# Token-major branches and gates, and state-space tables stored without a mask, in a two-block decoder kernel

## The chip, the cores and the metric

The kernel runs on one core of a Trainium2 chip. It is one program with one launch. The metric is the device time of one execution in microseconds; a profiled execution gives a trace of each engine's instructions beside it. The engines are TensorE (PE, with its weight loads PEld), the vector engine (DVE), ScalarE (ACT), GpSimd (POOL) and the queue of SyncE (SP), which issues most DMAs.

## The reference

256 tokens of width 2048 go through two blocks, in fp32. Cut to what the change touches:

```python
# block 1: three mixers, each with a gate of full width
gates = sigmoid(gate_logits).reshape(B, S, 3, D)           # from h @ w_in
mixed = (gates[:, :, 0] * (o_a @ w_branch_a) + gates[:, :, 1] * (o_b @ w_branch_b)
         + gates[:, :, 2] * (o_c @ w_branch_c))
x = x + rms_norm(mixed @ w_out, g_post_mix)
...                                                         # then a gated feed-forward layer
# block 2, first layer: a state-space mixer, 128 groups of 16 channels with 64 states
x_t = a * x_{t-1} + bb @ u_t;  y_t = Re(c @ x_t) + d * u_t  # an associative scan over 256 tokens
# block 2, second layer: attention with 16 heads in 4 groups, three branches each
o = sum over 3 branches of (sigmoid gate) * silu(z) * o_branch      # z from h @ w_qg
y = o.reshape(B, L, 2048) @ w_o
```

The three attention branches are attention over 15 compressed blocks, over selected blocks and over a window; with 256 tokens the last two are causal attention with keys and values of their own.

## The kernel before

Every large product takes its fp32 weights from HBM in units of two rows of 128 and 512 columns (512 KB, tile `raw`). `unit` (line 173 on) loads one on SP's queue; `split` turns it into a rounded high half `whi` (ScalarE, line 156) and a remainder `wlo` (vector engine, line 157), and three matmuls per product (high by high, high by low, low by high) are done at TensorE's fast fp32 rate. There are 4 buffers of `raw` and 3 of each half. Activations live as `Act`: feature-major, 128 features on the partitions and 256 tokens beside, as high and low halves.

Two functions multiply. `ws` is feature-major: the weights are stationary, 256 tokens move, and the result has features on the partitions. `as_` is token-major: 128 tokens of the activations are stationary, 512 weight columns move, and the result has tokens on the partitions. Both work on a unit at a time and call `pump` after it, which lets side work advance: generators for attention, retention, the state-space tables and the modulation vectors (in the background, `BACK`), each of which yields a cost that is charged against a rate per unit. `late` holds functions that `as_` calls before its second or third unit (`do_late`); the feed-forward layer uses it to transpose its token-major result (`transpose_act`, line 796) into an `Act`. A scheduler orders each engine's instructions by a simulated timeline, so program order and order in the trace differ in detail.

- `branch` (line 805 on) runs once for each of the three mixers. For four blocks of 512 columns it computes gates and the branch's product with `ws`, applies tanh on ScalarE, multiplies and adds into `mixed` (two tiles of 8 x 256), and for the last mixer splits the halved sum into the `Act` `mx`, which `post_norm` multiplies by `w_out`.
- `ssm_tables` (line 1124 on) builds the state-space tables beside the feed-forward layer. At its end eight steps multiply `bT` by the table `gm` (in DRAM, loaded 8 groups at a time by `group_tile`) into a PSUM tile whose four strips of 32 partitions are filled one after the other; ScalarE copies them, the vector engine adds the skip term, and GpSimd's queue writes `kern` (DRAM, 128 groups x (112 zeros + 16 x 128)), line 1297.
- `ssm` projects `u` (token-major) and then `z` (feature-major, 32 units). Beside the units of `z` run `ssm_states`, then `ssm_direct` and `ssm_scan` together, then `ssm_before` and `ssm_out`. `ssm_direct` (line 1577 on) loads each group's table from `kern` as overlapping windows, a Toeplitz matrix; in a row of 8 steps `s` the window runs into the channel before, so GpSimd multiplies the tile by the mask `past` (line 1588):

```python
nc.sync.dma_start(raw, bass.AP(tensor=self.kern.tensor, offset=self.kern.offset + g * 2160,
                               ap=[[16, 128], [2160, 8], [1, 128]]))
nc.gpsimd.tensor_mul(raw, raw, cols(past, 8))
```

- `ssm_scan` is a serial chain of 30 steps with four small vector instructions each (lines 1545 to 1548); `ssm_before` copies its result (line 1560), and `ssm_out` multiplies it by `gm`, loaded again.
- `nsa` multiplies, for each of four head groups, three blocks of gates `z` by the attention's outputs, feature-major; `nsa_attention` runs one group ahead as side work and leaves its outputs feature-major, with the values (`vc`, `vsw`) stationary and 4 x 128 columns of transposed probabilities moving.

GpSimd's instructions run in order, its DMA issues among them: after the last write of `kern` it multiplies `y` by the norm's gain (line 938) at the end of the feed-forward layer, and then makes the low halves of the first weights of `ssm` (`as_first`).

Of the kernel before, what the change touches and what calls it, by code (L numbers as in the profile page):

```python
# [17 lines left out]
OP = mybir.AluOpType  # L18
# [55 lines left out]
class Kernel:  # L74
# [115 lines left out]
    def ws(self, act, wv, c0, j=None, before=None, quiet=False, shared=False):  # L190
# [3 lines left out]

        nk = act.n
        ps = [self.mp.tile([128, 2, S], F32, name=f"mm{i}") for i in range(2)]
        for k0 in range(0, nk, 2):
# [8 lines left out]
            if before is None and not quiet:  # L206
                self.pump()
        return ps
# [596 lines left out]
    def branch(self, i, o, w, mixed, act=None, done=None):  # L805

        nc = self.nc
        win = self.a["w_in"].rearrange("o (k p) n -> p (o k) n", p=128)
        wv = w.rearrange("o (k p) n -> p (o k) n", p=128)
        for b in range(4):  # L810
            ps = self.ws(self.hT, win, GATE + i * D + b * 512)
            gs = []
            for q in range(2):
                g = self.work([128, 2, S], "big")
                nc.scalar.activation(g, ps[q], AF.Tanh, scale=0.5)
                gs.append(g)
            ps = self.ws(o, wv, b * 512)
            for q in range(2):
                k = b * 4 + q * 2
                m = mixed[k // 8].t[:, k % 8:k % 8 + 2]  # L820
                g = gs[q]
                if act is None:
                    nc.vector.scalar_tensor_tensor(m, g, 1.0, ps[q], op0=OP.add, op1=OP.mult)
                else:
                    nc.vector.scalar_tensor_tensor(g, g, 1.0, ps[q], op0=OP.add, op1=OP.mult)
# [169 lines left out]
    def first(self):  # L995
# [25 lines left out]
        mixed = [self.slot([128, 8, S], F32, "mixed") for _ in range(2)]  # L1021
# [29 lines left out]
        for m in mixed:  # L1051
            m.free()
        self.BACK = 0.2
        xs, h2, ready, ss = self.post_norm(mx, a["w_out"], a["g_post_mix"], a["x"][0])
# [70 lines left out]
    def ssm_tables(self):  # L1125
# [9 lines left out]
        self.kern = dp.tile([128, 112 + 16 * 128], F32, name="kern")  # L1135
# [109 lines left out]
        nc.gpsimd.dma_start(self.kern[:, :112], zero)  # L1245
# [37 lines left out]

        for t in range(8):
            p = self.ps([128, 4, 128], "sc", 1)
            for l in range(4):
                if l % 2 == 0:
                    raw = self.group_tile(self.gm.rearrange("g r n w -> g (r n) w"), t * 16 + l * 4)
                for q in range(4):
                    self.mm(p[l * 32:l * 32 + 16, q], bT.t[:, :, t * 16 + l * 4 + q], raw[:, l % 2 * 4 + q], True, True)  # L1290
            k = self.work([128, 4, 128], "side")
            for l in range(4):
# [3 lines left out]
                dst = self.kern[t * 16 + l * 4:t * 16 + l * 4 + 4, 112:]  # L1296
                nc.gpsimd.dma_start(dst.rearrange("q (c w) -> c q w", c=16), k[r])
# [687 lines left out]
```

## Time and profile before

| | |
|---|---|
| median of 3 runs (lowest, highest) | 3266.39 us (3265.74, 3269.41) |
| the profiled execution's own time | 3265.34 us |
| its span, first to last instruction | 3263.2 us |
| mean granted TensorE clock | 0.989 |
| HBM read, written | 716.80 MB, 24.24 MB |

A profile line gives a group of instructions by line, engine and operation, what it writes from what, and how often; then busy time, mean time of one, and the idle time of the engine before it with what ended it. In the timeline equal instructions in a row are merged (x4) under the start of the first and the time from there to the end of the last. Matmuls are pipelined: a record lasts longer than the distance to the next start. An fp32 product that is not in halves shows as two records.

### The profile page before, as it was taken

Reading aid. Unit: us, or ns where it says so; the run is one execution under the profiler, and the core shown is the slowest. Engines: PE = TensorE matmul, PEld = TensorE weight load, DVE = VectorE, ACT = ScalarE, POOL = GpSimd, SP = SyncE. Lnnn points to the kernel's source line nnn. Section 1 sums busy time; section 2 is a strip of 40 time slices with the busy share of each in tenths; the row PEclk is TensorE's granted clock in tenths of the full one; section 3 lists DMA queues with packets and bytes.
Section 4 is the critical chain, followed back from the end, with each engine's and each line's share of the span. In section 5 each row is a group of like instructions: output and inputs, shape, how many; then the busy total and the mean of one; then the engine's idle time right before and its main releaser. Section 6 shows DMA issues by size and latency. Waiting matters only on the chain. (4 is left out here: it accounts for less than half of the span.)

```text
span 3263.2 us, 52186 instructions
## 1 busy us (share of the span) xinstructions
PE 3166.2 (97%) x20582; PEld 2812.7 (86%) x20582; DVE 2375.1 (73%) x3580; ACT 1461.9 (45%) x2066; POOL 177.2 (5%) x184
## 2 busy tenths in 40 slices
PE   9999999999999998999999999898899899999998
PEld 8999899988999996887778778677798798899997
DVE  7777676777787766999989956757777865655666
ACT  5544434344344445444434444554444434544444
POOL 0000000000000002000000010303100200000000
PEclk9999999999999999999999999898999999999999
DMA  8868756888777785677777788486788585455574
GB/s 280 260 196 270 237 184 200 255 279 270 223 235 246 249 286 160 213 273 251 262 264 272 253 279 272 139 273 199 232 240 268 170 272 174 135 150 161 143 229 171
DMA packets 438246, 744.48 MB, mean 228 GB/s; under 512 B 29732, under 2 KB 105288, under 8 KB 437104
## 3 DMA queue, kind: packets, MB, share of 16 engines
q1 hardware_dynamic: 428000, 710.45, 68.4%
q0 software_dynamic: 9360, 29.62, 2.6%
q8 instruction: 161, 2.64, 0.3%
q10 hardware_dynamic: 640, 1.07, 0.1%
q14 instruction: 85, 0.70, 0.1%
HBM read 716.80 MB, written 24.24 MB: 227 GB/s over the span
## 5 line engine op out<-in xcount | busy, mean ns | idle before, releaser
L156 ACT CAST whi<-raw 128x1024 fp32r<-128x1024 f32 (+2 forms) x1059 | 1029.5, 981 | 1375.8 <-PE mm L150 1191.3
L157 DVE TENSOR_TENSOR wlo<-raw,whi 128x1024 fp32r<-128x1024 f32 (+2 forms) x1045 | 1181.6, 1139 | 611.3 <-ACT whi L156 600.0
L150 PE MATMUL mm<-act,whi 128*128 128x256 f32 (+1 forms) x8000 | 1485.0, 287 | 3.7 <-ACT whi L156 3.7
L150 PEld LDWEIGHTS mm<-act,whi 128*128 128x128 f32 (+1 forms) x8000 | 1255.5, 193 | 34.7 <-issue 24.3
L150 PE MATMUL mm<-whi,act 128*128 128x512 f32 x3792 | 1185.1, 391 | 5.4 <-ACT whi L156 4.5
L150 PE MATMUL mm<-act,wlo 128*128 128x256 f32 (+1 forms) x4000 | 1143.7, 288 | 7.0 <-DVE wlo L157 6.9
L150 PEld LDWEIGHTS mm<-whi,act 128*128 128x128 f32 x3792 | 711.4, 188 | 160.6 <-issue 7.0
L150 PEld LDWEIGHTS mm<-act,wlo 128*128 128x128 f32 (+1 forms) x4000 | 767.9, 193 | 23.9 <-issue 11.9
L150 PE MATMUL mm<-wlo,act 128*128 128x512 f32 x1896 | 743.9, 393 | 13.6 <-DVE wlo L157 11.6
L150 PEld LDWEIGHTS mm<-wlo,act 128*128 128x128 f32 x1896 | 356.6, 188 | 98.2 <-DVE wlo L157 21.3
L1087 DVE SCALAR_TENSOR_TENSOR acc<-side_raw,c_act,acc 128x512 f32<-128x512 f32 x480 | 359.3, 749 | 23.2 <-DMA side_raw<-mod_w 18.4
L150 PE MATMUL mm<-kept,act 128*128 128x512 f32 x360 | 95.0, 411 | 9.3 <-DVE act L157 9.3
L150 PEld LDWEIGHTS mm<-kept,act 128*128 128x128 f32 x360 | 69.1, 197 | 25.5 <-DVE act L157 10.9
L1273 DVE TENSOR_TENSOR side<-tables,ssm_c 128x512 f32<-128x512 f32 x64 | 65.7, 1088 | 2.3 <-DMA ssm_c<-ssm_c_re 2.3
L1107 POOL DMA_DIRECT2D mod<-side x24 | 12.0, 499 | 959.9 <-ACT side L1106 958.6
L156 ACT CAST kept<-raw 128x1024 fp32r<-128x1024 f32 x30 | 31.2, 1049 | 27.8 <-DMA raw<-w_out 7.4
L1588 POOL TENSOR_TENSOR side_raw<-side_raw,past 128x1024 f32<-128x1024 f32 x16 | 39.5, 2479 | 60.7 <-PE mm L150 33.5
L160 DVE SCALAR_TENSOR_TENSOR act<-tp,vec,act 128x256 fp32r<-128x256 f32 (+1 forms) x64 | 25.4, 413 | 22.3 <-ACT act L159 21.9
L150 PEld LDWEIGHTS tp<-diag,x 128*128 128x128 f32 x192 | 27.7, 205 | 15.1 <-issue 9.8
L150 PE MATMUL tp<-diag,x 128*128 128x128 f32 x192 | 29.0, 292 | 11.3 <-DVE diag L363 9.0
L159 ACT ACTIVATE act<-tp,vec 128x256 fp32r<-128x256 f32 (+1 forms) x64 | 25.5, 418 | 28.2 <-DVE act L160 13.4
L346 ACT ACTIVATE big<-x 128x512 f32<-128x512 f32 x40 | 25.1, 628 | 27.2 <-DVE x L1640 18.5
(378 smaller groups left out, 1929.8 us busy)
## 6 DMA issues: line engine op xcount, KB each, us to landing
raw<-w_in SPq DMA_DIRECT2D x272, 512.0 KB, 4.5
side_raw<-mod_w SPq DMA_DIRECT2D x192, 512.0 KB, 5.2
raw<-w_ffn_in SPq DMA_DIRECT2D x176, 512.0 KB, 5.0
raw<-nsa_w_qg SPq DMA_DIRECT2D x128, 512.0 KB, 3.7
raw<-w_ffn_out SPq DMA_DIRECT2D x88, 512.0 KB, 5.3
side_raw<-kv_mod_w SPq DMA_DIRECT2D x64, 512.0 KB, 4.7
raw<-ssm_w_in SPq DMA_DIRECT2D x64, 512.0 KB, 5.0
raw<-w_kv SPq DMA_DIRECT2D x48, 512.0 KB, 4.4
```

Of the source, the lines that this page charges most:

```text
L150: return self.nc.tensor.matmul(out, lhsT, rhs, start=start, stop=stop, skip_group_check=True).ins
L156: self.last_hi = nc.scalar.copy(hi, src).ins
L157: self.last = (engine or nc.vector).tensor_sub(lo, src, hi.bitcast(F32)).ins
L159: nc.scalar.activation(hi, src, AF.Copy, scale=scale)
L160: self.last_scaled = nc.vector.scalar_tensor_tensor(lo, src, scale, hi.bitcast(F32), op0=OP.mult, op1=OP.subtract).ins
L346: return self.nc.scalar.activation(self.work([128, 512], "big"), x, AF.Square, accum_out=out).ins
L1087: nc.vector.scalar_tensor_tensor(acc, raw[:, k], c, acc, op0=OP.mult, op1=OP.add)
L1107: nc.gpsimd.dma_start(flat[n:n + 4].rearrange("(o k) p -> o (k p)", o=1), row[r])
L1273: nc.vector.tensor_mul(w[i], y[r][:, :, :, None].to_broadcast([128, 4, 8, 16]), x[q][:, :, None, :].to_broadcast([128, 4, 8, 16]))
L1588: nc.gpsimd.tensor_mul(raw, raw, cols(past, 8))
```

## The change

Three things are changed together.

1. `branch` uses `as_` for gates and products. `mixed` becomes two tiles of tokens x 2048, tanh, products and additions work on tokens x 512, and for the last mixer the sum is transposed into `mx` by TensorE, through `late`. `ws` calls `do_late` too, after its second unit. The tiles of `mixed` are freed through `late`.
2. The gates of `nsa` use `as_` as well. `nsa_attention` leaves its outputs token-major: the probabilities are stationary and the values move, four products of 128 columns in place of one of 512. The sum of a group is transposed into `o` through `late`.
3. `kern` gets 112 zeros ahead of each channel (16 x 240 a group), so that windows need no mask. After each step of the table build, 16 copies from DRAM to DRAM on GpSimd's queue, one a group, write the windows out as `direct`, and `ssm_direct` loads its tile from there in one plain DMA. The mask and its product go. The loads of `gm` in the table build are fetched up to three ahead, and its products alternate between two strips.

```diff
 def ws(...):                          # after the matmuls and pump of a unit
+            if k0 == 2:
+                self.do_late()
 def branch(...):
-            ps = self.ws(self.hT, win, GATE + i * D + b * 512)
+            c = slice(b * 512, b * 512 + 512)
+            ps = self.as_(self.hT, win, GATE + i * D + b * 512)
             gs = []
-            for q in range(2):
-                g = self.work([128, 2, S], "big")
-                nc.scalar.activation(g, ps[q], AF.Tanh, scale=0.5)
+            for t in range(2):
+                g = self.work([128, 512], "big")
+                nc.scalar.activation(g, ps[t], AF.Tanh, scale=0.5)
                 gs.append(g)
-            ps = self.ws(o, wv, b * 512)
+            ps = self.as_(o, wv, b * 512)
...
-                if done is not None:
-                    self.split(done.hi(k, 2), done.lo(k, 2), m, 0.5)
+            if done is not None:
+                self.late.append(partial(self.transpose_act, [m.t[:, c] for m in mixed], done, 4, b * 4, 0.5))
 def ssm_tables(...):
-        self.kern = dp.tile([128, 112 + 16 * 128], F32, name="kern")
+        self.kern = dp.tile([128, 16, 240], F32, name="kern")
+        self.direct = dp.tile([16, 128, 8, 128], F32, name="direct")
...
-        nc.gpsimd.dma_start(self.kern[:, :112], zero)
+        nc.gpsimd.dma_start(self.kern[:, :, :112], cols(zero, 16))
...
+        get = self.fetched(partial(self.group_tile, self.gm.rearrange("g r n w -> g (r n) w")), range(0, 128, 8))
         for t in range(8):
             p = self.ps([128, 4, 128], "sc", 1)
-            for l in range(4):
-                if l % 2 == 0:
-                    raw = self.group_tile(self.gm.rearrange("g r n w -> g (r n) w"), t * 16 + l * 4)
+            for l0 in range(0, 4, 2):
+                raw = get()
                 for q in range(4):
-                    self.mm(p[l * 32:l * 32 + 16, q], bT.t[:, :, t * 16 + l * 4 + q], raw[:, l % 2 * 4 + q], True, True)
+                    for l in range(l0, l0 + 2):
+                        self.mm(p[l * 32:l * 32 + 16, q], bT.t[:, :, t * 16 + l * 4 + q], raw[:, l % 2 * 4 + q], True, True)
...
             yield 1.5
+            for g in range(t * 16, t * 16 + 16):
+                src = bass.AP(tensor=self.kern.tensor, offset=self.kern.offset + g * 3840, ap=[[240, 16], [16, 8], [1, 128]])
+                nc.gpsimd.dma_start(self.direct[g // 8, :, g % 8].rearrange("(c s) w -> c s w", s=8), src)
+            yield 0.1
 def ssm_direct(...):
-            nc.sync.dma_start(raw, bass.AP(tensor=self.kern.tensor, offset=self.kern.offset + g * 2160,
-                                           ap=[[16, 128], [2160, 8], [1, 128]]))
-            nc.gpsimd.tensor_mul(raw, raw, cols(past, 8))
+            nc.sync.dma_start(raw, self.direct[g // 8])
 def nsa(...):
-                ps = self.ws(h, wq, D + 48 + br * D + g * 512)
+                ps = self.as_(h, wq, D + 48 + br * D + g * 512)
...
+            self.late += [partial(self.transpose_act, [acc[:, t] for t in range(2)], o, 4, g * 4, 0.5), self.Q[g].free]
 def nsa_attention(...):
-            self.mm(o.rearrange("p h t -> p (h t)"), self.vc[:15, g], pT[:15].rearrange("p h t -> p (h t)"), True, True)
+            for h in range(4):
+                self.mm(o[:, h], pT[:15, h], self.vc[:15, g], h == 0, True)
...
-                    self.mm(o.rearrange("p h t -> p (h t)"), self.vsw.t[:, br, m, g * 128:g * 128 + 128],
-                            pT.rearrange("p h t -> p (h t)"), m == 0, m == t)
+                    for h in range(4):
+                        self.mm(o[:, h], pT[:, h], self.vsw.t[:, br, m, g * 128:g * 128 + 128], m == 0 and h == 0, m == t)
```

## Rows read from the trace of the kernel before

**Rows 1.** The page, busy us (share of the span) and instructions.

```profile
PE 3166.2 (97%) x20582; PEld 2812.7 (86%) x20582; DVE 2375.1 (73%) x3580; ACT 1461.9 (45%) x2066; POOL 177.2 (5%) x184
```

**Rows 2.** Stretches: us, busy time of each engine, PEclk, DMA share, GB/s.

```profile
900.00:1000.00 100.00, 100.00 (x794) 96.84 (x793) 79.99 (x165) 41.40 (x49) 0.97 (x2) 1.00 0.74 228
...
1400.00:1600.00 200.00, 196.38 (x869) 159.18 (x868) 186.17 (x207) 84.35 (x90) 8.76 (x16) 1.00 0.75 260
...
2200.00:2400.00 200.00, 168.96 (x1655) 151.77 (x1654) 141.78 (x229) 85.13 (x125) 42.17 (x21) 0.91 0.75 222
...
2800.00:3000.00 200.00, 200.00 (x1508) 183.79 (x1508) 122.67 (x220) 99.06 (x174) 0.00 (x0) 1.00 0.52 147
```

**Rows 3.** Timeline (start, us) of TensorE, a feature-major unit in a branch.

```profile
1060.19 0.40 PE L150 MATMUL mm<-act,whi 128*128 128x256 f32 x2
...
1063.07 0.40 PE L150 MATMUL mm<-act,whi 128*128 128x256 f32 x2
```

**Rows 4.** Timeline, a token-major unit of the feed-forward layer.

```profile
1508.38 0.62 PE L150 MATMUL mm<-whi,act 128*128 128x512 f32 x2
...
1511.10 0.62 PE L150 MATMUL mm<-whi,act 128*128 128x512 f32 x2
```

**Rows 5.** Timeline of TensorE, transposes among feed-forward matmuls.

```profile
1334.15 0.60 PE L796 MATMUL tp<-ident,big 128*128 128x128 f32 x4
...
1335.05 0.40 PE L150 MATMUL mm<-wlo,act 128*128 128x512 f32 x1
```

**Rows 6.** Timeline of TensorE, an output product of the second block's attention.

```profile
2773.62 1.02 PE L150 MATMUL pv<-side,vsw 128*128 128x512 f32 x2
...
2774.72 0.28 PE L150 MATMUL mm<-act,wlo 128*128 128x256 f32 x1
```

**Rows 7.** Timeline of TensorE, fp32 products of 128 columns.

```profile
103.34 1.95 PE L150 MATMUL tp<-diag,x 128*128 128x128 f32 x16
...
105.36 0.63 PE L150 MATMUL mm<-whi,act 128*128 128x512 f32 x2
```

**Rows 8.** Timeline of TensorE, one step of the table build.

```profile
1943.13 2.46 PE L150 MATMUL sc<-side_raw,ssm_bT 128*16 128x128 f32 x32
```

**Rows 9.** Timeline of TensorE, products that go round four strips.

```profile
2226.20 0.64 PE L150 MATMUL sc<-side_raw,uT 128*32 128x128 f32 x16
```

**Rows 10.** Timeline, the vector engine and GpSimd in the state-space stage.

```profile
2268.13 0.28 DVE L1548 TENSOR_TENSOR state<-state,half 128x128 f32<-128x128 f32 x1
...
2271.76 9.87 POOL L1588 TENSOR_TENSOR side_raw<-side_raw,past 128x1024 f32<-128x1024 f32 x4 [7.75 <-DMA side_raw<-kern]
2272.11 2.43 DVE L1547 TENSOR_TENSOR state<-state,half 128x128 f32<-128x128 f32 x1
```

**Rows 11.** The chain of waits in that stage (start, us, what).

```profile
2291.50 2.36 DVE state L1547
...
2353.97 10.73 DMA side_raw<-gm
```

**Rows 12.** DMA queues from 1910 to 1980: packets, MB, share of 16 engines.

```profile
q1 hardware_dynamic: 20062, 19.40, 84.9%
q0 software_dynamic: 960, 0.92, 3.9%
```

**Rows 13.** DMA issues of the page: count, size, us to landing.

```profile
kern<-side POOLq DMA_DIRECT2D x32, 32.0 KB, 5.1
```

**Rows 14.** Groups by line, GpSimd's DMA issues: busy us, mean ns.

```profile
L1297 POOL DMA_DIRECT2D kern<-side x32 | 16.4, 514 | 68.9 <-DVE side L1295 67.2 <-issue 0.3
L1279 POOL DMA_DIRECT2D gm<-ssm_ring x16 | 10.9, 681 | 234.5 <-DVE ssm_ring L1278 234.5
```

**Rows 15.** Timeline of GpSimd, first and last of eight steps, and what follows.

```profile
1910.79 2.06 POOL L1297 DMA_DIRECT2D kern<-side  x4 [18.28 <-DVE side L1295]
...
1976.47 2.33 POOL L1297 DMA_DIRECT2D kern<-side  x4 [8.03 <-DVE side L1295]
2047.98 1.28 POOL L938 TENSOR_TENSOR y<-y,gb 128x512 f32<-128x512 f32 x1 [69.17 <-ACT big L346]
```

More of the change, by code (lines that the diff above doesn't have):

```diff
@@ L1020, in first @@
         self.finish(att)
-        mixed = [self.slot([128, 8, S], F32, "mixed") for _ in range(2)]
+        mixed = [self.slot([128, D], F32, "mixed") for _ in range(2)]
         oa = Act(self, 8)
@@ L1050, in first @@
         self.hT.free()
-        for m in mixed:
-            m.free()
         self.BACK = 0.2
+        self.late += [m.free for m in mixed]
         xs, h2, ready, ss = self.post_norm(mx, a["w_out"], a["g_post_mix"], a["x"][0])
@@ L1752, in nsa @@
             o.grow()
-            acc = self.Q[g].t[:, 0]
+            acc = self.by_token(g)
             for br in range(3):
-                ps = self.ws(h, wq, D + 48 + br * D + g * 512)
-                for j in range(2):
-                    z = self.work([128, 2, S], "big")
-                    self.twice_silu(z.rearrange("p a t -> p (a t)"), ps[j].rearrange("p a t -> p (a t)"))
-                    m = acc[:, 2 * j:2 * j + 2]
+                ps = self.as_(h, wq, D + 48 + br * D + g * 512)
+                for t in range(2):
+                    z = self.work([128, 512], "big")
+                    self.twice_silu(z, ps[t])
+                    m = acc[:, t]
                     if br == 0:
@@ L1762, in nsa @@
                         continue
-                    nc.vector.tensor_mul(z, z, self.P[g].t[:, br - 1, 2 * j:2 * j + 2])
+                    nc.vector.tensor_mul(z, z, self.P[g].t[:, br - 1, t])
                     nc.vector.tensor_add(m, m, z)
-                    if br == 2:
-                        k = g * 4 + 2 * j
-                        self.split(o.hi(k, 2), o.lo(k, 2), m, 0.5)
-            self.Q[g].free()
             self.P[g].free()
+            self.late += [partial(self.transpose_act, [acc[:, t] for t in range(2)], o, 4, g * 4, 0.5), self.Q[g].free]
         h.free()
@@ L1875, in nsa_attention @@
         scale = 128 ** -0.5
-        self.P[g] = self.slot([128, 2, 4, S], F32, "pv")
+        self.P[g] = self.slot([128, 2, 2, 512], F32, "pv")
         q, out = self.Q[g].t[:, 1], self.P[g].t
+        first = self.by_token(g)
         p = self.ps([128, 2, 4, 15], "sc", 1)
@@ L1904, in nsa_attention @@
             o = self.ps([128, 4, 128], "pv", 1)
-            self.mm(o.rearrange("p h t -> p (h t)"), self.vc[:15, g], pT[:15].rearrange("p h t -> p (h t)"), True, True)
-            nc.scalar.copy(self.Q[g].t[:, 0, :, t * 128:t * 128 + 128], o)
+            for h in range(4):
+                self.mm(o[:, h], pT[:15, h], self.vc[:15, g], h == 0, True)
+            nc.scalar.copy(first[:, t], o.rearrange("p h d -> p (h d)"))
         yield
@@ L1934, in nsa_attention @@
                     nc.scalar.copy(pT, pt)
-                    self.mm(o.rearrange("p h t -> p (h t)"), self.vsw.t[:, br, m, g * 128:g * 128 + 128],
-                            pT.rearrange("p h t -> p (h t)"), m == 0, m == t)
-                nc.scalar.copy(out[:, br, :, t * 128:t * 128 + 128], o)
+                    for h in range(4):
+                        self.mm(o[:, h], pT[:, h], self.vsw.t[:, br, m, g * 128:g * 128 + 128], m == 0 and h == 0, m == t)
+                nc.scalar.copy(out[:, br, t], o.rearrange("p h d -> p (h d)"))
                 yield
@@ L1975 @@
     arrays["decay"] = decay_table()
-    arrays["past"] = past_table()
     nc = bacc.Bacc("TRN2", target_bir_lowering=False, num_devices=1)
```

22 lines of the change are left out of this document (8 added, 14 removed).

## The prediction

> **What bounds the kernel now.** I read the page's busy times first. TensorE is at 97% of the span, the vector engine at 73%, GpSimd at 5% [rows 1]. Busy TensorE is no proof of a bound, because matmul ends are modelled, so I next read the table of stretches. The reader is to see three kinds there. In the branches (900 to 1000 us) and in the second block's attention (2800 to 3000) TensorE is full and the vector engine is not, at 80% and 61%. In the feed-forward part (1400 to 1600) it is at 196 of 200 us although the vector engine is at 93%. Only from 2200 to 2400, in the state-space part, has it real gaps: 169 of 200 us, and a mean granted clock of 0.91 [rows 2]. So a change to the first two kinds is worth what it changes in TensorE's own issue time, and the third kind must be read from its waits.
>
> The timeline gives the issue time. In a feature-major unit (`ws`) the weights are stationary and 256 tokens move: 24 matmuls start between 1060.19 and 1063.07, so 2.88 us a unit, 120 ns each [rows 3]. In a token-major unit (`as_`) the activations are stationary and 512 weight columns move: 12 matmuls from 1508.38 to 1511.10, so 2.72 us, 227 ns each [rows 4]. Both do the same products of the same two weight rows.
>
> **Part 1: the branches and the attention's gates become token-major.** The branches have 3 x 4 blocks with 8 units of gates each (96), and 4 x (4 + 8 + 4) = 64 units of branch weights; the attention's gates have 4 x 3 x 8 = 96. These 256 units go from 2.88 to 2.72 us: 256 x 0.16 = 41 us less. Neither side work nor weight loads per unit change. The cover is the vector engine: a stretch at 80% that gets 5.6% shorter is at 85%, and the feed-forward part shows that this form of unit keeps TensorE at 98% with the vector engine at 93% [rows 2]. By the Trainium skill (TensorE: Matmul & The Clock Gate, Back-to-back issue gap) an isolated matmul takes N/2.4 + 2.5 ns; 24 x 109 ns and 12 x 216 ns differ by 0.03 us a unit, which is an estimate of 8 us in place of 41. The trace does not agree for its pairs of weight load and 256-column matmul: they start every 120 ns.
>
> The sum is now token-major, so it has to be transposed: 8 transposes for each of the last branch's 4 blocks and for each of the 4 attention groups, 64 in all. Four transposes among feed-forward matmuls start at 1334.15; two matmuls after them the next one starts at 1335.05, and 0.90 less two times 0.227 leaves 0.45, so 0.112 us each [rows 5]: +7 us. They run two units after the sum is made, by `late`, and I cost their wait at nothing: two units are 5.4 us. If the vector engine is late by 2 us each time, eight places cost 16 us; that is kept for the range. Tanh, products and splits stay as many and as large.
>
> The attention's output products turn round as well. Each 512-column fp32 product is two records and holds TensorE from 2773.62 to about 2774.48 (2774.72 less two 120 ns matmuls), 0.86 us [rows 6]. In its place come four products of 128 columns, eight records. Sixteen such records run from 103.34 to 105.13 (105.36 less one 227 ns matmul), 0.112 us each [rows 7], so four products take 0.90 us. There are 8 + 24 of them: 32 x 0.04 = +1 us.
>
> **Part 2: the table build.** The products with `ssm_bT` have 16 stationary columns, and all of one `l` go to one strip of the array: 32 records in 2.46 us; less the 0.28 us of the last one that is 0.070 us apart [rows 8]. The change alternates two strips. A stretch that goes round four strips (`uT`) has 16 records in 0.64 us, 0.023 us apart [rows 9]. So the 256 records lie between no gain and 12 us; two strips are half of four, and I take 0.040, -8 us. TensorE is the bound in that stretch, so it counts.
>
> Added are 128 copies from `kern` to `direct`, 64 KB each in 512-byte rows, on GpSimd's queue, and a zero fill 16 times as large. No DRAM-to-DRAM copy stands in the trace. GpSimd's time for one issue is bounded by the issues that it has, 0.51 and 0.68 us [rows 14]; I take 0.55, because `kern`'s own writes are the nearest. A step is then four writes (2.1 us), the wait for their landing (5.1 us, [rows 13]) and 16 x 0.55 = 8.8 us: 16 us, where steps now come every 9.4 us ((1976.47 - 1910.79)/7, [rows 15]). So the copies fall behind and end 8 x 16 = 128 us after the first write, at about 2039 by the old clock. GpSimd's next task stands at 2047.98 [rows 15], so they are just hidden. Queued behind them are that product with the norm's gain and then the weight splits of the state-space input, for which TensorE waits; each us past 2048 costs about one.
>
> The copies also take the DMA engines. From 1910 to 1980 those are at 84.9% for the SP queue. The POOL queue moved 960 packets for 3.9% of 16 x 70 us, 45 ns each [rows 12]. 16,384 new packets at 45 ns are 46 us of all 16 engines, spread over some 128 us: 0.36 on top of 0.85. The sum passes 1, so weights land later; four raw buffers (four units, 11 us) absorb the bursts. Below, this costs nothing; above, the excess of 0.2 x 128 = 26 us. I take +5, nearer to nothing, since after 1980 the steps of the table build no longer load `gm` too.
>
> **Part 3: no mask in the state-space part.** Sixteen GpSimd products of 2.5 us go. What is to be seen is the vector engine beside them: a scan addition takes 0.28 us alone, and 2.43 us beside the four GpSimd products that run from 2271.76 in 9.87 us, 2.47 each [rows 10]. So each product holds the vector engine for some 2.15 us more, 16 x 2.15 = 34 us, in a stretch where that engine is the chain: the chain there consists of such pieces of 2.4 us and then, when the output products follow, of `gm` loads of up to 10.7 us [rows 11]. The Trainium skill (SBUF — State Buffer, on the shared port pair) says that the two engines lock one pair of ports for a whole instruction; the trace agrees with 2.43 us. The loads of the tables become 4 KB rows instead of 512 bytes. I take -30 us. Below: 12, a third of it, if the `gm` loads end the stage whatever comes before. Above: 55, if the scan ends so early that the output products run under the projection's matmuls.
>
> **The sum**: -41 + 7 + 1 - 8 - 30 + 5 = -66 us. The profiled execution took 3265.34 us (span 3263.2), 1 us under the median of the runs shown, 3266.39. 3265.3 - 66 = **3200 us** (rounded).
>
> **The rivals.**
> *A. The stage is bound by its loads.* With the mask gone, the chain of `gm` loads after 2328 stays where it is [rows 11]; the gain there is 12, not 30: 3218 us. For it speaks that such a load takes 10.7 us there; against it, that the loads can start earlier when the scan ends earlier.
> *B. The copies crowd the weights.* 26 instead of 5: 3221 us. For it: 0.85 + 0.36; against: bursts have 6 to 7 us of pause while GpSimd waits for landings.
> *C. The copies block GpSimd's queue: slower.* Place: the queue from the first step to the state-space input. Were each copy to wait until the one before has landed, 128 x 5.1 us + 8 x 7.2 us = 710 us stand where 137 are free (1911 to 2048): 3200 + 570 = 3770 us. It decides early: above (137 - 8 x 7.2)/128 = 0.62 us a copy the queue is late, and above 0.62 + 66/128 = 1.14 us a copy the kernel is slower than before. For it: 0.62 is close to 0.55, and the copies of eight groups write one tensor in alternate rows. Against: `kern`'s four writes of one step leave in 2.06 us, so they don't wait for each other [rows 15]. The Trainium skill (SBUF — State Buffer, the trap of DVE and SWDGE) adds that GpSimd can't write descriptors while the vector engine runs in a two-port mode; in this trace the issues keep their 0.51 us on average [rows 14].
> *D. The change of form gives little.* A token-major unit needs its low weights at its second matmul, a feature-major one at its third. Should each unit wait one 120 ns matmul for them, 256 x 0.12 = 31 us are lost and 10 remain: 3231 us. For it: the vector engine makes the low weights and gets busier. Against it: the feed-forward part runs this form without such gaps [rows 2].
> *E. More overlap than I count.* 55 in the state-space stage: 3175 us.
>
> **How the numbers follow.** Forecast (3190 to 3210) 0.47; A 0.17; B 0.11; C 0.08; D 0.05; E 0.12. The predicted time is the forecast's. The range takes in E, A, B and D with their own scatter: 3163 to 3236 us, which leaves out C and little else. About 0.2% (6.5 us) is what a measurement of this kernel can tell from no change. All cases but C are faster by more; C's mild forms, and A, B and D falling together, put 0.03 on no change: faster 0.90, same 0.03, slower 0.07.
>
> **What would show it.** Right: matmuls of 512 columns in the branches and the attention, 2.72 us a unit, and no idle time before the 64 transposes; `ssm_bT` records about 0.04 us apart; GpSimd's copies at 0.5 to 0.6 us each, ending before the product at line 938; scan additions at 0.28 us throughout; the stretch that was 2230 to 2390 about 30 us shorter. Wrong: GpSimd's copies above 0.65 us, TensorE waiting for `raw` weights or for GpSimd's splits after the feed-forward part, or the `gm` chain as long as before.

## The result, and the profile after

The changed kernel takes 3215.7 us (median of 4 runs, 3213.72 to 3218.46) where the one before took 3267.9 us in the same session: ratio 0.9839, 95% interval 0.9822 to 0.9856. The forecast was 3200 us with a range of 3163 to 3236. The time fell by 52 us where the sum said 66. The profiled execution took 3217.06 us (3265.34 before), its span is 3215.2 us, and the mean granted clock is 0.989 as before.

The page's busy times, which answer to [rows 1], and its row of the copies (busy us, mean ns, idle time of GpSimd before them):

```profile
PE 3128.3 (97%) x17766; PEld 2663.2 (83%) x17766; DVE 2348.2 (73%) x3580; ACT 1461.8 (45%) x2066; POOL 205.0 (6%) x296
...
L1307 POOL DMA_DIRECT2D direct<-kern x128 | 66.9, 543 | 25.0 <-DMA direct<-kern 14.4
```

To see where the time went I use the issue times of loads as milestones: a weight load is issued when a buffer comes free, so it follows TensorE's progress. The rows give shortest, median and longest issue in ns, then the first and last start. Before:

```profile
L180 SPq DMA_DIRECT2D raw<-w_out x32: 367/368/379, 1166.0 to 1248.1; - x32
L180 SPq DMA_DIRECT2D raw<-w_ffn_out x88: 367/368/388, 1404.8 to 2038.1; - x88
L1379 POOL DMA_DIRECT2D u<-big x8: 557/561/679, 2097.4 to 2192.8; - x8
L180 SPq DMA_DIRECT2D raw<-ssm_w_out x32: 367/368/368, 2448.7 to 2529.6; - x32
L180 SPq DMA_DIRECT2D raw<-w_kv x48: 367/368/682, 2532.2 to 2730.1; - x48
L180 SPq DMA_DIRECT2D raw<-nsa_w_qg x128: 367/368/390, 2680.1 to 3148.2; - x128
```

After:

```profile
L180 SPq DMA_DIRECT2D raw<-w_out x32: 367/368/378, 1146.6 to 1228.7; - x32
L180 SPq DMA_DIRECT2D raw<-w_ffn_out x88: 367/368/929, 1386.0 to 2015.8; - x88
L1389 POOL DMA_DIRECT2D u<-big x8: 547/560/599, 2087.4 to 2181.8; - x8
L180 SPq DMA_DIRECT2D raw<-ssm_w_out x32: 367/368/382, 2407.5 to 2488.1; - x32
L180 SPq DMA_DIRECT2D raw<-w_kv x48: 367/368/1052, 2490.8 to 2690.2; - x48
L180 SPq DMA_DIRECT2D raw<-nsa_w_qg x128: 367/368/393, 2639.8 to 3100.0; - x128
```

| stretch, from these starts | before | after | moved | the prediction's terms |
|---|---|---|---|---|
| start to first load of `w_out` (branches) | 1166.0 | 1146.6 | -19.4 | -22 |
| to last load of `w_ffn_out` (feed-forward, table build) | 872.1 | 869.2 | -2.9 | -3 |
| to first write of `u` (the passage) | 59.3 | 71.6 | **+12.3** | 0 |
| to first load of `ssm_w_out` (state-space stage) | 351.3 | 320.1 | -31.2 | -30 |
| to first load of `w_kv` | 83.5 | 83.3 | -0.2 | 0 |
| to last load of `nsa_w_qg` (attention) | 616.0 | 609.2 | -6.8 | -11 |

These add up to -48.2 us, the 48 us by which the span of the profiled execution fell. (-22 is 160 of the 256 units at 0.16 us and 32 transposes; -11 the rest of that part.) Four stretches do about what was forecast. The passage got longer, and its 12.3 us are most of the 18 that are missing; the attention lacks 4.

The terms in the rows of after. A branch unit [rows 3, 4] in TensorE's timeline; 13 matmuls start between 1059.65 and 1062.60, 0.227 us each, so 2.72 us a unit. Behind it stand eight transposes of the sum, with no idle time noted:

```profile
1059.65 0.39 PE L150 MATMUL mm<-whi,act 128*128 128x512 f32 x1
...
1061.92 0.84 PE L150 MATMUL mm<-whi,act 128*128 128x512 f32 x3
1062.60 0.39 PE L150 MATMUL mm<-wlo,act 128*128 128x512 f32 x1
...
1121.83 1.03 PE L799 MATMUL tp<-ident,mixed 128*128 128x128 f32 x8
1122.62 0.48 PE L150 MATMUL mm<-wlo,act 128*128 128x512 f32 x1
```

The table products [rows 8]: 32 records in 1.54 us, and (1.54 - 0.28)/31 = 0.041 us apart (0.040 forecast).

```profile
1921.92 1.54 PE L150 MATMUL sc<-side_raw,ssm_bT 128*16 128x128 f32 x32
```

One of the scan's four lines, grouped from 2190 to 2300 us: 290 ns on average where single ones took 2.43 us [rows 10].

```profile
L1555 DVE TENSOR_TENSOR half<-state,tables 128x128 f32<-128x128 f32 x30 | 8.7, 290 | 0.8
```

GpSimd's timeline of the passage answers to [rows 15]:

```profile
2024.40 1.38 POOL L941 TENSOR_TENSOR y<-y,gb 128x512 f32<-128x512 f32 x1 [26.93 <-ACT big L349]
2030.53 1.29 POOL L941 TENSOR_TENSOR y<-y,gb 128x512 f32<-128x512 f32 x1 [4.75 <-ACT big L349]
2031.76 8.37 POOL L1307 DMA_DIRECT2D direct<-kern  x16
2040.02 4.76 POOL L157 TENSOR_TENSOR kept<-raw,kept 128x1024 fp32r<-128x1024 f32 x2
```

112 of the 128 copies are issued before 1998, and GpSimd then stands idle for 27 us. The last sixteen come only after the norm's first two products, and the weight splits (`kept`) of the state-space input stand behind them.

### The profile page after: what moved, and what is told of

Its sections match the earlier page's. It is cut to its first block, busy times and chain, and to the rows that moved or that the text cites. A ratio compares the mean times of both kernels' runs of the same rounds, so it can differ in the third digit from the quotient of the medians.

```text
span 3215.2 us, 46687 instructions
## 1 busy us (share of the span) xinstructions
PE 3128.3 (97%) x17766; PEld 2663.2 (83%) x17766; DVE 2348.2 (73%) x3580; ACT 1461.8 (45%) x2066; POOL 205.0 (6%) x296
## 5 line engine op out<-in xcount | busy, mean ns | idle before, releaser
L150 PE MATMUL mm<-whi,act 128*128 128x512 f32 x5840 | 1834.1, 393 | 4.9 <-ACT whi L156 4.2
L150 PEld LDWEIGHTS mm<-whi,act 128*128 128x128 f32 x5840 | 1096.0, 188 | 246.0 <-issue 12.3
L150 PE MATMUL mm<-wlo,act 128*128 128x512 f32 x2920 | 1152.7, 395 | 14.2 <-DVE wlo L157 12.8
L150 PE MATMUL mm<-act,whi 128*128 128x256 f32 x3904 | 720.9, 286 | 3.9 <-ACT whi L156 3.9
L150 PEld LDWEIGHTS mm<-wlo,act 128*128 128x128 f32 x2920 | 550.0, 188 | 142.2 <-DVE wlo L157 23.3
L150 PEld LDWEIGHTS mm<-act,whi 128*128 128x128 f32 x3904 | 609.8, 192 | 18.1 <-issue 9.9
L150 PE MATMUL mm<-act,wlo 128*128 128x256 f32 x1952 | 551.7, 286 | 2.5 <-DVE wlo L157 2.5
L150 PEld LDWEIGHTS mm<-act,wlo 128*128 128x128 f32 x1952 | 372.3, 192 | 7.1 <-DVE wlo L157 4.5
L1307 POOL DMA_DIRECT2D direct<-kern x128 | 66.9, 543 | 25.0 <-DMA direct<-kern 14.4
L150 PE MATMUL tp<-diag,x 128*128 128x128 f32 x192 | 31.8, 312 | 20.9 <-DVE diag L366 14.8
L156 ACT CAST kept<-raw 128x1024 fp32r<-128x1024 f32 x30 | 31.2, 1050 | 29.2 <-DMA raw<-w_out 7.3
```

The costliest lines, as they stand in the source:

```text
L150: return self.nc.tensor.matmul(out, lhsT, rhs, start=start, stop=stop, skip_group_check=True).ins
L156: self.last_hi = nc.scalar.copy(hi, src).ins
L1307: nc.gpsimd.dma_start(self.direct[g // 8, :, g % 8].rearrange("(c s) w -> c s w", s=8), src)
```

## The experiments

My theory: the form of the units gives some -27 us, the mask's end some -30, and the copies cost 12 in the passage, through GpSimd's queue. Twelve runs, each timed in five rounds against the kernel before. Feed-forward, passage and stage are the stretches of the table above, from each run's profile. One profile is one execution, so its stretches scatter: the one ahead of `w_out` lies between 1145.4 and 1147.8 us in the twelve kernels with token-major branches, and the feed-forward stretch between 867.1 and 870.2 in the seven that build the tables as the changed kernel does, but for the place of the last copies. The passage is 71.4 to 72.5 us in the five with sixteen copies ahead of the splits, and 55.4 to 61.7 in the six with none.

| kernel | ratio to before (95%) | feed-forward | passage | stage |
|---|---|---|---|---|
| before | 1 | 872.1 | 59.3 | 351.3 |
| changed | 0.9839 (0.9822 to 0.9856) | 869.2 | 71.6 | 320.1 |
| `form_only` | 0.9917 (0.9903 to 0.9930) | 873.1 | 57.5 | 354.1 |
| `tables_only` | 0.9938 (0.9926 to 0.9951) | 871.4 | 72.0 | 325.8 |
| `mask_back` | 0.9930 (0.9918 to 0.9943) | 868.0 | 71.4 | 351.0 |
| `mask_aside` | 0.9928 (0.9916 to 0.9941) | 870.2 | 72.5 | 348.5 |
| `nocopy8` | 0.9958 (0.9946 to 0.9971) | 870.1 | 61.7 | 370.8 |
| `one_strip` | 0.9848 (0.9834 to 0.9861) | 876.6 | 72.2 | 319.3 |
| `half_copies` | 0.9803 (0.9790 to 0.9817) | 875.4 | 55.4 | 322.2 |
| `copies_late` | 0.9779 (0.9765 to 0.9792) | 867.1 | 56.9 | 320.3 |
| `ahead_4` | 0.9814 (0.9800 to 0.9827) | 870.0 | 59.5 | 326.1 |
| `ahead_6` | 0.9810 (0.9797 to 0.9823) | 869.6 | 62.1 | 317.0 |
| `late_8` | 0.9830 (0.9817 to 0.9844) | 868.0 | 61.5 | 326.4 |
| `late_four` | 0.9770 (0.9756 to 0.9783) | 867.2 | 55.8 | 315.9 |

**The two halves alone.** The diff's parts, each on the kernel before: `form_only` keeps its changes to `ws`, `branch`, `nsa` and `nsa_attention`; `tables_only` those to `ssm_tables` and `ssm_direct`.

> The kernel before with part 1 alone: branches, their gates and the attention's gates token-major, the tables and the mask as before. Theory (the parts add up, read from the first weight loads of the traces: branches -19.4, attention -7.9): -27 us, about 3241, ratio 0.9917, the state-space stage as long as before. Prediction's own terms for this part: -41 + 7 + 1 = -33 us. Rival D (a token-major unit waits for its low weights): -10 us or less, 3258. Rival (the parts help each other, since later work then meets earlier transfers): outside of -24 to -30.

> The kernel before with parts 2 and 3 alone: two strips in the table build, the copies, no mask; branches and attention as before. Theory: table build -2.4, passage from the feed-forward part to the state-space part +13, state-space stage -29.4 and what follows it -2, together about -21 us, 3247, ratio 0.9936. Prediction's own terms: -8 + 5 - 30 = -33 us. Rival (the parts meet in time: the passage's loss comes from the earlier end of the branches and the shifted order, not from the copies): -30 us or more, with the passage as short as before, 38 us.

Measured: 0.9917 is -27 us, 0.9938 is -20 us. The parts add (-47 against -52 for both, within the intervals). The long passage comes with the tables: 72.0 us there, 57.5 in `form_only`, so it is not the earlier end of the branches that makes it. Rival D is out: the form alone gives far more than 10 us.

**The mask's product, put back and put aside.**

```diff
 # mask_back, in load() of ssm_direct; `one` is a tile of ones
             nc.sync.dma_start(raw, self.direct[g // 8])
+            nc.gpsimd.tensor_mul(raw, raw, cols(one, 8))
 # mask_aside, in its place
+            for i in range(0, 8, 4):
+                nc.gpsimd.tensor_mul(self.work([128, 4, 128], "side"), raw[:, i:i + 4], cols(one, 4))
```

> The changed kernel with a GpSimd product put back on each tile of tables, by a tile of ones, so that its data stay as they are. Theory (GpSimd's product locks the vector engine out): scan additions beside it back to some 2.4 us, the state-space stage longer by 29 us, 3245 us; of the 29, 16 x 2.15 = 34 us is the most that the lock explains. Rival A (loads set the end of the stage): +12 us at most, 3228, with the chain of gm loads at its old place. Rival (the 4 KB rows of the new loads, not the mask, gave the gain): under +8 us, 3224 or less.

> As the run with the mask's product put back, but GpSimd now writes its products into two tiles that nobody reads (32 products of 512 columns in place of 16 of 1024), so that TensorE's table products no longer wait for GpSimd. The output is as before. Theory (GpSimd's instructions hold the vector engine, whose scan is the chain): most of the 31 us of that run stay, the stage from the first write of u to the first load of ssm_w_out 340 to 351 us in place of 320, time 3236 to 3245. Rival (the mask costs because the tables come ready 2.5 us later and TensorE waits): the stage at 320 to 326 us, time 3216 to 3222.

Both lose nearly all that the mask's end gave: stage 351.0 and 348.5 us. They keep the loads in 4 KB rows, so these are not what gave it. In `mask_back` TensorE also waits for GpSimd's tile; in `mask_aside` no instruction waits for the product, and the loss is nearly the same. TensorE waits 10.4 us there for loads of the tables (1.3 in the changed kernel), whose buffers GpSimd's product reads too, but most of the loss is seen in the scan itself. Its four lines in `mask_aside`, 2190 to 2330:

```profile
L1557 DVE TENSOR_TENSOR state<-state,half 128x128 f32<-128x128 f32 x30 | 16.2, 539 | 0.0
L1556 DVE TENSOR_TENSOR half<-state,tables 128x128 f32<-128x128 f32 x30 | 16.2, 539 | 0.0
L1555 DVE TENSOR_TENSOR half<-state,tables 128x128 f32<-128x128 f32 x30 | 14.9, 497 | 0.7
L1558 DVE TENSOR_TENSOR state<-state,half 128x128 f32<-128x128 f32 x30 | 12.5, 417 | 0.7
```

59.8 us where the changed kernel has 34.4 (8.7 + 8.7 + 8.5 + 8.5): 25 of the 28 us are in these 120 instructions. The kernel before has 59.0 (17.0 + 16.3 + 12.9 + 12.8), so they hold 25 of the 31 us of the change as well. The Trainium skill (SBUF — State Buffer, Who interferes with whom) says that a vector instruction with two SBUF inputs contends with a GpSimd instruction that reads SBUF; the runs agree.

**No copies.** The tile is loaded from the padded rows in eight pieces.

```diff
-            nc.sync.dma_start(raw, self.direct[g // 8])
+            for i in range(8):
+                src = bass.AP(tensor=self.kern.tensor, offset=self.kern.offset + (g + i) * 3840, ap=[[240, 16], [16, 8], [1, 128]])
+                nc.sync.dma_start(raw[:, i], src)
```

> The changed kernel without the copies: the padded rows stay, and each tile of the state-space part is loaded straight from them, in eight loads of 64 KB on SP's queue in place of one of 512 KB. Theory (GpSimd's last sixteen copies stand in its queue ahead of the weight splits of the state-space input): the passage from the last feed-forward matmul to the first write of u goes from 51 us back to about 38, so -13 us if the eight loads cost nothing, 3203; if the loads in 512-byte rows lengthen the state-space stage by up to 8 us, -5 us, 3211. Rival B (the copies' share is DMA traffic): the passage stays near 51 us, and what comes back is spread over 1890 to 2035 us, some 5 us. Rival (the passage is long because TensorE comes to it earlier than the DMA or the vector engine can serve): passage stays at 51 us, time unchanged or longer.

The passage came back as the theory has it, to 61.7 us, but the stage took 370.8: I had put the loads' price at 8 us at most, and it was 51. The row of these loads:

```profile
L1590 SPq DMA_DIRECT2D side_raw<-kern x128: 514/597/1352, 2210.3 to 2295.8; - x128
```

128 issues fill SP's queue for 85 us, 0.67 each, and the weights are behind them: ScalarE waited 24.3 us for loads of `ssm_w_in`, in the changed kernel not at all. How the rest of the 51 comes about was not traced. So the copies buy plain loads; they are not to be dropped but to be placed.

**The last sixteen copies, later.** The sixteen copies of a step become a function, `copies(t)`; `copies(7)` is taken out of the last step and issued after the first write of `u` and its read-back:

```diff
+            if t < 7:
+                self.copies(t)
...
+            if q == 0:
+                with self.tc.issue_after(there.ins):    # there: the last read-back of u
+                    self.copies(7)
```

> The changed kernel with the last sixteen of the 128 copies issued later on GpSimd's queue: behind the first write of u and its read-back, in place of ahead of the first weight splits of the state-space input. Nothing else is moved. Theory (those sixteen issues, 8.4 us, stand ahead of the splits for which TensorE waits): from the last load of w_ffn_out to the first write of u 60 us in place of 71.6, the whole kernel 10 to 12 us faster than the changed one, some 3204 us, ratio 0.981. Rival (the copies slow the passage through DMA or memory, or through the 112 that come before): the passage stays at 68 to 72 us and the time at 3213 to 3219. Rival (the loads of the tables now wait for the late copies): the passage is short, the state-space stage longer by as much.

0.9779: 3198.2 us, some 20 us below the changed kernel (0.0060 of 3268) where 10 to 12 were expected, and below the kernel before with a wide margin. The spans differ by 19.6 us: 14.7 from the passage, the rest in pieces of 1 to 2 us. The stage keeps its length (320.3 for 320.1), so the loads of the tables do not wait for the late copies. TensorE's timelines in the passage, with the idle time before each row; the changed kernel first, `copies_late` second:

```profile
2045.03 2.05 PE L150 MATMUL tp<-diag,x 128*128 128x128 f32 x8 [8.64 <-DVE diag L366]
2048.27 2.07 PE L150 MATMUL tp<-diag,x 128*128 128x128 f32 x8 [1.20 <-DVE bit L338]
...
2054.30 2.08 PE L150 MATMUL tp<-diag,x 128*128 128x128 f32 x8 [3.52 <-DVE half L1360]
2057.30 2.08 PE L150 MATMUL tp<-diag,x 128*128 128x128 f32 x8 [0.93 <-DVE half L1360]
...
2072.48 2.08 PE L150 MATMUL tp<-diag,x 128*128 128x128 f32 x8 [6.19 <-DVE diag L366]
```

```profile
2041.94 2.05 PE L150 MATMUL tp<-diag,x 128*128 128x128 f32 x8 [8.24 <-DVE diag L366]
2044.67 2.07 PE L150 MATMUL tp<-diag,x 128*128 128x128 f32 x8 [0.68 <-DVE bit L338]
2046.39 3.54 PE L150 MATMUL mm<-kept,act 128*128 128x512 f32 x8
```

I had thought that TensorE waits for the splits; in this passage it does not. It waits for the norm's diagonal matrices (`diag`), which the vector engine makes. The first wait is in all three kernels: 8.64 us in the changed kernel, 8.24 in `copies_late`, 7.55 in the kernel before. What the changed kernel has besides is a second one, 6.19 us, for the matrix of the second 128 tokens, and one of 3.52 us for the vector engine's `half`; `tables_only` has the same, 5.82 and 3.52. The granted clock of 2040 to 2060 was 0.50, its lower level of 1.2 GHz, after the first wait; in `copies_late` it was at 0.52 for 2040 to 2050 and back at 1.00. Both kernels' rows of `diag` on the vector engine, the changed one first, with four steps that lead to its second matrix:

```profile
2038.54 6.34 DVE L366 TENSOR_SCALAR diag<-ident,bit 128x128 f32<-128x128 f32 x1
...
2061.13 3.61 DVE L963 SCALAR_TENSOR_TENSOR x<-y,bit,x 128x512 f32<-128x512 f32 x2
...
2065.53 1.47 DVE L376 SCALAR_TENSOR_TENSOR bit<-bit 128x1 f32<-128x1 f32 x1 [0.54 <-ACT big L349]
...
2067.73 1.57 DVE L344 SCALAR_TENSOR_TENSOR bit<-bit 128x1 f32<-128x1 f32 x1
...
2069.65 1.95 DVE L344 SCALAR_TENSOR_TENSOR bit<-bit 128x1 f32<-128x1 f32 x1
...
2072.14 0.28 DVE L366 TENSOR_SCALAR diag<-ident,bit 128x128 f32<-128x128 f32 x1
```

```profile
2039.46 2.33 DVE L366 TENSOR_SCALAR diag<-ident,bit 128x128 f32<-128x128 f32 x1
...
2062.89 0.29 DVE L366 TENSOR_SCALAR diag<-ident,bit 128x128 f32<-128x128 f32 x1
```

The first ends at 2044.88, right after the two GpSimd splits that start at 2040.02; its first 1.5 us lie beside the last copies' issues. It costs little against `copies_late`, where the same instruction takes 2.33 us beside one split and two steps before it 1.97 and 1.95: the waits of TensorE differ by 0.4 us. The second matrix takes 0.28 us, but it starts 56.3 us after the last load of `w_ffn_out`, where `copies_late` needs 50.3. The four steps shown before it took 8.6 us; their counterparts in `copies_late` took 1.9 (1.41, 0.20, 0.15, 0.14). GpSimd's splits run beside them, from 2061.79 to 2071.59. So a part of the 6 us is again the vector engine held by GpSimd; how much of it is the order alone was not separated.

**How many may stay ahead.** Of the sixteen, eight, six and four are left in the last step and the others go late; with eight:

```diff
-            if t < 7:
-                self.copies(t)
+            self.copies(t, 16 if t < 7 else 8)
...
-                    self.copies(7)
+                    self.copies(7, 16, 8)
```

> As the run with the last sixteen copies late, but eight of them stay ahead of the splits (4.2 us of issues) and eight go late. If the passage grows with the time for which GpSimd's queue is held: halfway, 64 us from the last load of w_ffn_out to the first write of u (71.6 with sixteen, 56.9 with none), time some 3206. Rival (the first 4 us are covered, and what costs is the later part): 57 to 60 us, 3199. Rival (whatever stands there breaks the order of the splits and TensorE's clock falls for as long): 69 to 72 us, 3213.

> Four of the last sixteen copies stay ahead of the splits, twelve go late. In this kernel TensorE's instructions of the passage stand in the same order as before: twelve products with the kept weights between the first two sets of transposes of the state-space input (with eight copies ahead it was one product, with sixteen one as well). If the order is what costs: as with none ahead, from the last load of w_ffn_out to the first write of u 56 to 59 us, time 3196 to 3202. If the time on GpSimd's queue costs, in proportion to the copies: the four take a quarter of what sixteen did (3.7 us of 14.7) and half of what eight did, so 3202 to 3206.

> Six ahead, ten late. TensorE's order has seven products in place of twelve between the first two sets of transposes. If the order costs: a second wait for the second diagonal matrix of some 4 us, half of the 7.6 us that eight ahead showed, time 3201 to 3207. If time on the queue costs in proportion: 3203 to 3208 and no second wait.

The passage is 56.9, 59.5, 62.1, 61.5 and 71.6 us with none, four, six, eight and sixteen ahead. GpSimd's rows with eight:

```profile
2030.33 4.22 POOL L1313 DMA_DIRECT2D direct<-kern  x8
2036.01 9.28 POOL L157 TENSOR_TENSOR kept<-raw,kept 128x1024 fp32r<-128x1024 f32 x4 [1.46 <-ACT kept L156]
```

GpSimd is free 1.46 us before ScalarE lets it start the splits, so with eight (and with six and four: 2.51 and 3.55 us) its queue is not late for these splits. Yet TensorE waits for the second matrix, 7.60 us with eight, 5.42 with six, 1.28 with four, none with none. With eight:

```profile
2047.66 0.77 PE L150 MATMUL mm<-kept,act 128*128 128x512 f32 x1
2049.03 2.08 PE L150 MATMUL tp<-diag,x 128*128 128x128 f32 x8 [0.60 <-DVE half L1364]
...
2068.40 2.08 PE L150 MATMUL tp<-diag,x 128*128 128x128 f32 x8 [7.60 <-DVE diag L366]
```

The order is another one: one product with the kept weights between the sets of transposes where `copies_late` has twelve (2046.39 x8 and four more). The scheduler orders each engine by its simulated timeline, in which, as I take it, the copies push the splits back. The first half's transposes then come earlier, their evictions stand on the vector engine ahead of the second half's norm, and `diag` starts 53.6 us after the last load of `w_ffn_out` in place of 50.3. Here too steps before it are held: 3.52 and 1.83 us for the first two of the four shown above. That fits the order theory, which no run tests by itself. Four copies ahead, with the order of before, have a passage 2.6 us longer than none, where I expected 0 to 2. With none ahead it lies between 55.4 and 61.7, `nocopy8` included, which has no copies; so what four, six or eight cost in the passage is not clear of scatter; what sixteen cost is.

The whole times don't follow the passage alone: four ahead should have been within 4 us of none by the order theory and was 11 us slower. 5.8 of the 12.7 us between the two profiles lie in the stage, where a copy on ScalarE's queue waits for the read-back of `u`, with weight splits behind it. In `ahead_4`:

```profile
2121.85 4.05 ACT L1491 COPY u_group<-u_chunk 64x1024 f32<-64x1024 f32 x2 [8.00 <-DMA u_chunk<-u]
...
2126.90 1.22 PE L150 MATMUL mm<-whi,act 128*128 128x512 f32 x2 [5.98 <-ACT whi L156]
```

That wait is 5.49 us with eight ahead, 4.07 with six, 3.90 in the changed kernel; `copies_late` has none there. It does not explain the stage: the changed kernel and `ahead_6` have this wait, and their stages, 320.1 and 317.0 us, are no longer than that of `copies_late` (320.3). Nor can one profile decide it: the five times of `ahead_6` lie between 3201.5 and 3212.1, and its profile is of the shortest. Why all three are slower than none by more than their passage stays open.

**Fewer, larger copies.** 64 copies of 128 KB, by `s` in place of by group:

```diff
+            to = self.direct.rearrange("(c s) g w -> s c g w", s=8)
+            for s in range(8):
+                src = bass.AP(tensor=self.kern.tensor, offset=self.kern.offset + t * 61440 + s * 16, ap=[[240, 16], [3840, 16], [1, 128]])
+                nc.gpsimd.dma_start(to[s, :, t * 16:t * 16 + 16], src)
```

> The changed kernel with 64 copies of 128 KB in place of 128 of 64 KB, the same bytes in the same 512-byte rows. All of them stand ahead of the norm's products on GpSimd's queue. Theory (what costs is the place of issues ahead of the splits): passage 60 us, total about 3204. If an issue takes as long as it has rows (some 1.1 us for 256), the copies take as long as before, and the last ones may still be waiting when the splits should start: 3208 to 3216. Rival (traffic): unchanged, since the bytes are the same.

```profile
L1308 POOL DMA_DIRECT2D direct<-kern x64: 563/563/584, 1901.2 to 1976.0; - x64
```

An issue costs 0.563 us with 256 rows where it cost 0.537 with 128 (medians), so here the price is per issue and hardly per row; the rival with 1.1 us is out. All copies end before the norm and the passage is 55.4 us. But the feed-forward stretch is 6.2 us longer: the same bytes come in 75 us (1901.2 to 1976.0), while the first seven eighths took the changed kernel 97 (1898.8 to 1996). ScalarE's waits for weights between 1880 and 2010, changed kernel first:

```profile
L156 ACT CAST whi<-raw 128x1024 fp32r<-128x1024 f32 x40 | 42.0, 1052 | 49.4 <-PE mm L150 41.5 <-DMA raw<-w_ffn_in 7.5 <-DVE side L1301 0.2
```

```profile
L156 ACT CAST whi<-raw 128x1024 fp32r<-128x1024 f32 x40 | 41.9, 1052 | 45.9 <-PE mm L150 28.3 <-DMA raw<-w_ffn_in 14.2 <-DVE acc L1089 2.7
```

This speaks for rival B as a dose: with the copies packed closer, ScalarE waits 6.7 us longer for weights; spread as in the changed kernel, these waits are no longer than in the kernel before (8.0). That they made the stretch longer is not shown: `late_four` below has nearly as long waits, with shorter table products, and its stretch is not longer.

**Strips.** `one_strip` takes the table products back to one strip at a time, as before; `late_four` has `copies_late` and goes round all four:

```diff
-            for l0 in range(0, 4, 2):
-                raw = get()
-                for q in range(4):
-                    for l in range(l0, l0 + 2):
+            raw = [get(), get()]
+            for q in range(4):
+                for l in range(4):
```

> The changed kernel with the table products back in the order of before, all of one l on one strip. Theory: the 256 records go from 0.041 us apart back to 0.070, and TensorE is the bound there: +7 us, 3223, ratio 0.986. Rival (they lie beside waits, or something else bounds that stretch): no change, within 2 us.

> The last sixteen copies late, as in the run that does only this, and the table products round all four strips. Theory: 256 records from 0.041 to 0.023 us apart, -4.6 us, on top of the -11 of the late copies: about 3200 us, ratio 0.979. Rival (two tiles of gm are wanted at once, so TensorE waits for loads in that stretch): no gain over the run with the late copies alone, or a loss of some us.

`one_strip`: 32 records in 2.46 us again, and the feed-forward stretch is 876.6 in place of 869.2 us, +7.4 for a term of 8; by the ratio it is 3 us slower with intervals that overlap, so the size rests on the profiles. `late_four`: 32 records in 1.22 us at best, 0.030 us apart, and 0.0009 less than `copies_late`, which the intervals don't tell apart; ScalarE's waits for `w_ffn_in` rose to 12.8 us, with a feed-forward stretch of 867.2. It is the fastest kernel run, 3195.9 us, by no margin that counts.

## Why the prediction was right, and what it missed

**Form of the units.** Right in mechanism and size: 2.72 us a unit, transposes unhidden but cheap (0.79 us for 8, 0.90 forecast), no wait at `late`. Of -33 for this part, -26 came (-19.4 and -6.8). A part of what the attention lacks is a cost that the sum did not have: an fp32 score product of 256 columns keeps TensorE longer among 512-column matmuls than among 256-column ones. The group's records, before and after:

```profile
L150 PE MATMUL sc<-kT,q 128*128 128x256 f32 x32 | 9.5, 379 | 0.0
```

```profile
L150 PE MATMUL sc<-kT,q 128*128 128x256 f32 x32 | 10.2, 401 | 0.0
```

From start to start, less the matmuls between, such a product took 0.43 us before. After, twelve of them stand among 512-column matmuls: four took some 0.56 us (those at 2707, 2714, 2886 and 2994) and eight some 0.46. The score products of 512 columns took 0.86 and 0.88. Together that is about 1 us of the 4.2 that are missing; the rest stays open, and why the four are dearer was not tested. What the branches lack (2.6 us) was not traced.

**Strips, copies' traffic, table build.** -8 and +5 were forecast, -2.9 came, but that the sum of the two comes out is luck. TensorE's busy time on the 256 table products fell from 20.9 to 14.7 us (1880 to 2010; 21.5 in `one_strip`), so the strips' term is there, a little small. The traffic's term is not: `nocopy8` has no copies at all, and its feed-forward stretch, 870.1 us, is no shorter than the 869.2 with them. The term was sized too large as well. It counted 16,384 packets; from 1890 to 2040 the POOL queue moved 5097 in the changed kernel and 1088 in `nocopy8`, and its share of the sixteen engines was 17.8% and 2.0% of 150 us, so the copies took 24 us of all engines and not 46. What took back the other 3 us of the strips' gain is open; `form_only`, which leaves the table build as it was, has a stretch 1.0 us longer than before.

**Mask.** -30 forecast, -31.2 came, and both runs with the product give it back. The step "each product holds the vector engine" was right: 25 of the 31 us are in the scan's own instructions. It was counted as 34 us for sixteen products and set to 30 by judgement, so the nearness of -31.2 is in part luck. A (loads set the end) and E (55) are out.

**The copies on GpSimd's queue: the step that failed.** The prediction had them "just hidden", ending at 2039 by the old clock just before the product at 2047.98, and named the weight splits as what is behind. They ran a little faster than counted: 112 of them were out by the new clock's 1998, 14 us a step and not 16. The error was to take the queue's order as the order of readiness. The last sixteen were placed behind the norm's first products, where their 8.4 us stand ahead of the splits. That cost +12.3 us, which no term held. It is a mild form of rival C's place with a mechanism of its own. It was not landing times: an issue took 0.54 us, and GpSimd waited 14.4 us in all for copies to land, ahead of the norm. It was not TensorE waiting for the splits either, which the prediction named as the way by which the queue would cost. What is seen is a second wait for `diag`, behind a vector engine that GpSimd's splits hold and an order that puts the second half late, and a stretch at the lower clock. Moving these sixteen alone took it back, to 3198.2 us, 2 us from the forecast. That nearness is in part luck: against the kernel before in its own session the fall is 72 us where the sum said 66, and 68 by the spans.

The measured 3215.7 us lies near the times of rivals A (3218) and B (3221), and neither is what happened. The range held because it had been made wide for them; the miss of 16 us has another cause.

## What to carry to other kernels

Where a scheduler fixes each queue's order, work added to a free queue is not hidden because there is room in time: look at what it stands next to, and pin it (here behind the first read-back of `u`) where nothing waits. An elementwise GpSimd instruction beside a serial vector chain can cost the chain much of its length, even if no one reads its result: here 44 us of GpSimd's products in `mask_aside` made the scan 25 us longer. When a part of the gain is missing, split the span at loads that follow the bounding engine, and compare stretch by stretch before forming a theory.

## What the runs showed of the hardware that was not expected

- A 128 x 128 vector instruction took 6.34 us in place of 0.28: its first 1.5 us beside the issues of GpSimd's last copies, the rest beside two GpSimd splits of 2.4 us. What held it in the first part is not known.
- DRAM-to-DRAM copies on GpSimd's queue cost 0.537 us an issue with 128 rows and 0.563 with 256. The Trainium skill (DMA: Bandwidth & Descriptors, Anatomy of one DMA) says that many descriptors can be emitted before their number costs; these two sizes agree with it.
- 64 KB loads with 512-byte rows took SP 0.67 us each to issue, 128 of them 85 us, where sixteen loads of 512 KB took 0.32 us each.
- Two strips in turn give 0.041 us between products with 16 stationary columns, four 0.030, one 0.070.
